# Low parts of routing weights: a GpSimd subtraction or an adding DMA

## The chip, the cores and the metric

The kernel runs on one core of one Trainium2 chip. The metric is the device time of that core in microseconds. Three runs of the kernel before took 2883.79 us in the median (2883.66 to 2886.31).

## The reference

Two blocks follow one another on 512 tokens of width 1024, all in float32. The first holds a layer with a gated convolution and a recurrent mixer, and a layer of sparse attention. The second holds a small mixer, the expert layer to which the change belongs, and a last gate. The expert layer, cut to what matters:

```
q = (xb @ w_q).reshape(T, 8, 2, 128)              # 8 heads, two queries of 128 each
s = jnp.einsum('thpd,hpkd->thpk', q, sub_keys)    # against 2 x 128 keys
sv, si = lax.top_k(s, 16)
cand = sv[:, :, 0, :, None] + sv[:, :, 1, None, :]     # 16 x 16 pairs
cidx = si[:, :, 0, :, None] * 128 + si[:, :, 1, None, :]
top_s, pos = lax.top_k(cand, 16)
eidx = jnp.take_along_axis(cidx, pos, axis=-1)    # 16 of 16384 experts a head
gate = softmax(top_s)
act = gelu(jnp.einsum('thkd,td->thk', expert_u[eidx], xb))
out = jnp.einsum('thk,thkd->td', gate * act, expert_v[eidx])
```

Each token takes 128 experts. An expert is a row of `expert_u`, a row of `expert_v` and a gate.

## The kernel before

**Split products.** TensorE multiplies each float32 matrix as two rounded parts. A weight `w` becomes a high part `wh` (`w` rounded to the matmul's format) and a low part `wl = w - wh`; the activations are split in the same way. `product()` (L214) then issues three matmuls for each k-tile of 128 rows: `wh`·`xh` (L216), `wh`·`xl` (L217) and `wl`·`xh` (L218). `proj()` (L231) runs over the k-tiles of one block of 128 output channels, `KR` of them for each piece of weight that `weight()` (L179) brings.

**Two ways to make the parts.** `weight()` has two branches. In the second one, which the routing stage uses before the change, SP's queue loads the piece as `wraw` (128x256, `KR` = 2, `RB` = 6 buffers; while the experts are routed one more of the name `wrawx` from the pool `wx`), ScalarE copies it to `wh` with rounding (L207), and GpSimd subtracts (L209). The first one is taken where `self.wd` is a pool: SP's queue loads `draw` (128x512, three buffers), ScalarE writes the rounded weight to `dh` (L190) and its negative, rounded too, to `dl` (L191), and a DMA that GpSimd issues (L192) reads the same weight from memory again and adds it to `dl` on arrival. `dh` and `dl` have four buffers each. The convolution stage at the start of the program uses it, with `KR` = 4; behind that stage it is switched off.

**The expert layer.** `peer()` (L1174) treats the first 352 tokens as a dense problem and the last 160 by gathering rows.

- *Routing.* `route()` (L1391) goes over 8 heads. Each has two query projections of 8 k-tiles (`wq2`), scores against the keys, the choice of 16 on VectorE (`tops`), the sums of pairs, and the selection of the indices by comparisons (VectorE L1469, GpSimd L1472, VectorE L1475 and L1476). From the second head on one *early expert* is computed for each projection (`ahead`, `UQ` = 1).
- *Early experts.* 32 of the 128 blocks of `expert_u` (`uT`, 8 k-tiles each) are multiplied before the expert loop: `u_phase` (L1188) runs the projection and a gelu (L1191), the result goes to memory (`ga`, L1200) and is read back later (L1222).
- *Gathered tokens.* `rows()` (L1327) issues an indirect DMA on GpSimd's queue for 128 rows of `expert_u` (`grow`, five buffers, 0.52 MB), VectorE multiplies and sums (L1345). 160 such steps and 160 for `expert_v` (L1361) are spread over the routing stage and the expert loop. `chosen()` (L1309) makes their indices (L1312, L1314).
- *One-hot stage.* The gates become a softmax (L1486 to L1493). Then 44 sets of eight tokens follow: two comparisons on VectorE (`o1` L1511 in float32, `ob` L1514 in bfloat16), the gates laid over one of them by ScalarE (L1519) and GpSimd (L1520), a product on TensorE (L1525), which ScalarE copies to `st` (L1528). SP's queue writes `st` to memory as `gs` (L1529), 11 times 2 MB.
- *Expert loop.* For 128 experts `g4`, four experts' gates, is read back from `gs` on ScalarE's queue (L1219), the gelu is multiplied by it (L1226), split (L241, L242), and multiplied by the block of `expert_v` (`vraw` L1233, `vh` L1236, `vl` on GpSimd L1240 or VectorE L1238), L1256 to L1258. The pool `vp` of this loop lies where the routing stage's pools have been.

**What sets the order.** The program is written in the order of this code, then class `Order` (L1559) reads its dependences, prices each instruction (`cost()`, L1586) and writes an order for every engine's queue by list scheduling; `impose()` (L1859) puts the instructions into it. A DMA of GpSimd is priced there at 1038 ns of GpSimd and by its bytes. The order is made anew for each program, so an edit in one place can move instructions on every engine.

Of the kernel before, what the change touches and what calls it, by code (L numbers as in the profile page):

```python
# [133 lines left out]
class Net:  # L134
# [247 lines left out]
    wi, wxn, wx = -1, 0, None  # L382
# [791 lines left out]
    def peer(self):  # L1174
        nc, tc, I = self.nc, self.tc, self.I
        self.pair.close()
        self.psum2 = None
        with ExitStack() as L:
            self.px = L.enter_context(tc.tile_pool(name="px", bufs=1, space=bass.MemoryType.PSUM))
            hp = L.enter_context(tc.tile_pool(name="hp3", bufs=1))  # L1180
            xh, xl = self.hilo(hp, 8, "x", self.TD)
            dr = L.enter_context(tc.tile_pool(name="pdr", bufs=1, space=bass.MemoryType.DRAM))
            gs = dr.tile([self.TD // 32, 128, 128, 32], F32, name="gs")
            ga = dr.tile([self.NS, 128, self.TD], F32, name="ga")
            self.gather_open(L)
            up = L.enter_context(tc.tile_pool(name="up", bufs=1))

            def u_phase(e, keep):  # L1188
                ps = self.proj(I["uT"][e], xh, xl)
                g = up.tile([128, self.TD], F32, name="ga", bufs=self.GA) if keep else ps  # L1190
                nc.scalar.activation(g, ps, AF.Gelu_apprx_tanh)  # L1191
                return g

            with ExitStack() as RT:
                self.wx, self.wxn = RT.enter_context(tc.tile_pool(name="wx", bufs=1)), self.PX
                early = sorted(range(128), key=lambda e: (e % 4 + 4 * (e // 4 % 2) * (e % 4 == 1), e))[:self.NS]

                def ahead():
                    for i, e in enumerate(early):
                        nc.scalar.dma_start(ga[i], u_phase(e, True))  # L1200
                        self.pull(self.GE)
                        yield
                ahead = ahead()
                self.route(RT, xh, xl, gs, ahead)
                for _ in ahead:
                    pass
                self.wxn = 0
            with ExitStack() as VP:
                vp = VP.enter_context(tc.tile_pool(name="vp", bufs=1))
                g4 = None  # L1210
                GV = self.GV

                def prep(e0):
                    nonlocal g4
                    wh, wl, vh, vl = [], [], [], []
                    for e in range(e0, min(128, e0 + GV)):
                        if e % 4 == 0:
                            g4 = vp.tile([128, self.TD // 32, 4, 32], F32, name="g4", bufs=2)
                            nc.scalar.dma_start(g4, gs[:, :, e:e + 4, :].rearrange("g k e t -> k g e t"))  # L1219
                        if e in early:  # L1220
                            g = up.tile([128, self.TD], F32, name="ga", bufs=self.GA)
                            nc.scalar.dma_start(g, ga[early.index(e)])  # L1222
                        else:
                            g = u_phase(e, False)
                        gv = g.rearrange("p (g t) -> p g t", t=32)
                        nc.vector.tensor_tensor(gv, gv, g4[:, :, e % 4, :], OP.mult)  # L1226
                        h = vp.tile([128, self.TD], F32R, name="wwh", bufs=self.BW)
                        l = vp.tile([128, self.TD], F32R, name="wwl", bufs=self.BW)
                        self.split(h, l, g)
                        wh.append(h)  # L1230
                        wl.append(l)
                        raw = vp.tile([128, 1024], F32, name="vraw", bufs=2)
                        nc.sync.dma_start(raw, I["ev"][e])  # L1233
                        h = vp.tile([128, 1024], F32R, name="vh", bufs=self.BV)
                        l = vp.tile([128, 1024], F32R, name="vl", bufs=self.BV)
                        nc.scalar.activation(h, raw, AF.Copy)  # L1236
                        if e % 8 in self.VD:
                            nc.vector.tensor_tensor(l, raw, h.bitcast(F32), OP.subtract)  # L1238
                        else:
                            nc.gpsimd.tensor_tensor(l, raw, h.bitcast(F32), OP.subtract)  # L1240
                            self.pool = self.last()
                        self.pull(self.GR)
                        vh.append(h)
                        vl.append(l)
                    return wh, wl, vh, vl

                nxt = prep(0)
                for e0 in range(0, 128, GV):
                    wh, wl, vh, vl = nxt
                    if e0 + GV < 128:  # L1250
                        nxt = prep(e0 + GV)
                    for m in range(8):
                        po = self.bank(("xu", "tp", "xu", "nb")[m % 4])[:, 0:self.TD]
                        s = slice(128 * m, 128 * m + 128)
                        for i in range(len(wh)):
                            nc.tensor.matmul(po, vh[i][:, s], wh[i], start=(i == 0), stop=False)  # L1256
                            nc.tensor.matmul(po, vh[i][:, s], wl[i], start=False, stop=False)  # L1257
                            nc.tensor.matmul(po, vl[i][:, s], wh[i], start=False, stop=(i == len(wh) - 1))  # L1258
                        xm = self.x[m][:, 0:self.TD]
                        nc.vector.tensor_tensor(xm, po, xm, OP.add)  # L1260
                self.pull(999)
                self.gather_close()
# [642 lines left out]
```

## Time and profile before

| | before |
|---|---|
| median of 3 runs | 2883.79 us (2883.66 to 2886.31) |
| the profiled execution | 2893.17 us, its span 2891.4 us |
| TensorE matmuls, weight loads | 2621.8 us (91% of the span), 2231.9 us (77%) |
| VectorE | 2247.7 us (78%) |
| ScalarE | 1474.0 us (51%) |
| GpSimd | 1852.7 us (64%) |
| moved by DMA | 552.23 MB, 191 GB/s in the mean |

Shares of busy time are means over the whole span. The expert layer lies between about 1460 and 2750 us. The stretches there have other limits than the mean tells, so the table by stretch in the first group of rows is the first thing to read. PE is TensorE, PEld its weight loads, DVE VectorE, ACT ScalarE, POOL GpSimd, SP SyncE; "ACTq" and "SPq" are the DMA queues of those engines.

### The profile page before, as it was taken

To read this page: it belongs to the slowest core of one execution; us is meant where nothing else is said; L and a number is where in the kernel's file an instruction comes from. 1 tells how busy PE (TensorE), PEld (TensorE's weight loads), DVE (VectorE), ACT (ScalarE), POOL (GpSimd) and SP (SyncE) were. 2 spreads that over 40 slices of the span, in tenths; PEclk is the share of its full clock that TensorE was granted. 3 is DMA by queue.
4 is the path that set the end of the run, shared out by engine and by line. 5 is a ranking of instruction groups with operands and counts; after the bars stand their busy time and mean duration, and the time that the engine had idled before them with its cause. 6 is when DMAs were issued, how large, how long until landed. Compare 5 with 4: busy or idle time off the path is not lost.

```text
span 2891.4 us, 45285 instructions
## 1 busy us (share of the span) xinstructions
PE 2621.8 (91%) x14523; PEld 2231.9 (77%) x14523; DVE 2247.7 (78%) x4338; ACT 1474.0 (51%) x3068; POOL 1852.7 (64%) x1942
## 2 busy tenths in 40 slices
PE   5788998879979999999999988769999999999996
PEld 3656655656757787877878787669999999999995
DVE  6688679896367999973669969978877778788865
ACT  6536546556635538975454347723333444433435
POOL 4535646452245553346657788869988899998963
PEclk9759888888989999999999999979999999999988
DMA  8635444445694231123334366699999999999971
GB/s 264 161 66 118 98 95 107 93 99 126 145 289 143 76 96 44 46 93 105 96 102 148 101 201 245 254 316 337 321 329 314 300 340 339 334 345 320 325 245 64
DMA packets 353440, 552.23 MB, mean 191 GB/s; under 512 B 60081, under 2 KB 239153, under 8 KB 351538
## 3 DMA queue, kind: packets, MB, share of 16 engines
q1 hardware_dynamic: 224690, 295.22, 32.1%
q0 software_dynamic: 64800, 201.88, 23.5%
q10 hardware_dynamic: 63712, 52.24, 5.7%
q8 instruction: 114, 1.87, 0.3%
q14 instruction: 124, 1.02, 0.1%
HBM read 507.76 MB, written 41.42 MB: 190 GB/s over the span
## 4 chain that ended last, share of the span: by engine, by line
PE 31%; DVE 11%; issue 4%; POOL 4%; DMA 2%; ACT 1%; DVEq 0%; POOLq 0%; ACTq 0%; SPq 0%
PE mm L216 5%; PE mm L218 5%; PE mm L217 5%; PE xu L1258 2%; PE xu L1256 2%; PE xu L1257 2%; PE tp L1256 1%; PE tp L1258 1%; POOL wl L209 1%; PE tp L1257 1%; PE nb L1258 1%; PE nb L1256 1%; POOL grow L1330 1%; PE nb L1257 1%; DVE o L1511 1%
## 5 line engine op out<-in xcount | busy, mean ns | idle before, releaser
L209 POOL TENSOR_TENSOR wl<-wraw,wh 128x256 fp32r<-128x256 f32 x937 | 776.7, 846 | 349.3 <-ACT wh L207 290.4
L207 ACT ACTIVATE wh<-wraw 128x256 fp32r<-128x256 f32 x937 | 367.5, 413 | 466.2 <-PE mm L217 235.1
L216 PE MATMUL mm<-xh,wh 128*128 128x352 f32 (+1 forms) x1464 | 512.1, 350 | 11.2 <-DVE wwl L242 3.5
L218 PE MATMUL mm<-xh,wl 128*128 128x352 f32 (+1 forms) x1464 | 506.1, 349 | 6.7 <-POOL wl L209 6.7
L217 PE MATMUL mm<-xl,wh 128*128 128x352 f32 (+1 forms) x1464 | 507.9, 348 | 2.7 <-DVE xl L287 1.8
L216 PEld LDWEIGHTS mm<-xh,wh 128*128 128x128 f32 x1464 | 278.7, 190 | 33.8 <-DVE gate L1544 4.3
L218 PEld LDWEIGHTS mm<-xh,wl 128*128 128x128 f32 x1464 | 277.4, 190 | 26.5 <-POOL wl L209 8.6
L217 PEld LDWEIGHTS mm<-xl,wh 128*128 128x128 f32 x1464 | 278.5, 190 | 24.2 <-DVE xl L287 3.8
L1240 POOL TENSOR_TENSOR vl<-vraw,vh 128x1024 fp32r<-128x1024 f32 x96 | 231.2, 2416 | 6.0 <-ACT vh L1236 4.4
L192 POOL DMA_DIRECT2D dl<-in_wev x114 | 102.4, 917 | 201.7 <-ACT dl L191 180.5
L1345 DVE SCALAR_TENSOR_TENSOR gscr<-grow,wide 128x1024 bf16<-128x1024 f32 x160 | 194.1, 1213 | 38.3 <-DMA grow<-in_ue,gidx 34.8
L216 PE MATMUL mm<-xh,dh 128*128 128x512 f32 x456 | 205.5, 453 | 14.9 <-ACT xh L355 9.6
L1361 DVE SCALAR_TENSOR_TENSOR wide<-grow,gdot,wide 128x1024 f32<-128x1024 f32 x158 | 202.3, 1280 | 12.3 <-DMA grow<-in_ev,gidx 11.2
L217 PE MATMUL mm<-xl,dh 128*128 128x512 f32 x456 | 202.7, 446 | 9.2 <-DVE xl L356 9.2
L218 PE MATMUL mm<-xh,dl 128*128 128x512 f32 x456 | 202.0, 446 | 9.1 <-DMA dl<-in_wev 9.1
L1330 POOL DMA_INDIRECT grow<-in_ue,gidx x160 | 161.1, 1007 | 64.7 <-DVE gscr L1345 31.1
L1256 PE MATMUL xu<-wwh,vh 128*128 128x352 f32 x512 | 167.4, 328 | 32.2 <-ACT wwh L241 28.0
L1330 POOL DMA_INDIRECT grow<-in_ev,gidx x160 | 157.4, 984 | 36.1 <-issue 23.5
L1258 PE MATMUL xu<-wwh,vl 128*128 128x352 f32 x512 | 167.4, 328 | 9.7 <-POOL vl L1240 7.7
L1191 ACT ACTIVATE mm<-mm 128x352 f32<-128x352 f32 x96 | 43.0, 448 | 253.0 <-PE mm L218 211.4
L1257 PE MATMUL xu<-wwl,vh 128*128 128x352 f32 x512 | 167.2, 327 | 0.4 <-DVE wwl L242 0.4
L780 DVE SCALAR_TENSOR_TENSOR x<-u,vec,x 128x512 f32<-128x512 f32 x152 | 165.6, 1089 | 2.4
(575 smaller groups left out, 6961.2 us busy)
## 6 DMA issues: line engine op xcount, KB each, us to landing
vraw<-in_ev SPq DMA_DIRECT2D x128, 512.0 KB
wraw<-in_uT SPq DMA_DIRECT2D x494, 128.0 KB
draw<-in_wev SPq DMA_DIRECT2D x114, 256.0 KB
dl<-in_wev POOLq DMA_DIRECT2D x114, 256.0 KB
gs<-st SPq DMA_DIRECT2D x11, 2048.0 KB
g<-gs ACTq DMA_DIRECT2D x32, 704.0 KB
wraw<-in_wod SPq DMA_DIRECT2D x156, 128.0 KB
adaw<-in_adaT SPq DMA_DIRECT2D x32, 512.0 KB
```

What stands on the lines that cost most here:

```text
L207: nc.scalar.activation(wh, raw[:, s], AF.Copy)
L209: nc.gpsimd.tensor_tensor(wl, raw[:, s], wh.bitcast(F32), OP.subtract)
L216: nc.tensor.matmul(ps, wh, xh, start=start, stop=False)
L217: nc.tensor.matmul(ps, wh, xl, start=False, stop=False)
L218: nc.tensor.matmul(ps, wl, xh, start=False, stop=stop)
L1240: nc.gpsimd.tensor_tensor(l, raw, h.bitcast(F32), OP.subtract)
L1256: nc.tensor.matmul(po, vh[i][:, s], wh[i], start=(i == 0), stop=False)
L1257: nc.tensor.matmul(po, vh[i][:, s], wl[i], start=False, stop=False)
L1258: nc.tensor.matmul(po, vl[i][:, s], wh[i], start=False, stop=(i == len(wh) - 1))
L1330: self.nc.gpsimd.indirect_dma_start(out=t, out_offset=None, in_=src, in_offset=bass.IndirectOffsetOnAxis(ap=self.gidx[i][:, k:k + 1], axis=0))
L1345: nc.vector.scalar_tensor_tensor(scr, u, 1.0, x, op0=OP.mult, op1=OP.mult, accum_out=self.gdot[i][:, k:k + 1])
L1361: nc.vector.scalar_tensor_tensor(acc, r, w, acc, op0=OP.mult, op1=OP.add)
```

## The change

For the routing stage the change takes the first branch of `weight()` in place of the second: the pool `wr` holds `draw`, `dh` and `dl`, and `KR` is 4. Behind the early experts it is switched off again. The extra buffer `wrawx` goes.

```diff
             with ExitStack() as RT:
-                self.wx, self.wxn = RT.enter_context(tc.tile_pool(name="wx", bufs=1)), self.PX
+                self.wd, self.KR = RT.enter_context(tc.tile_pool(name="wr", bufs=1)), 4
                 early = sorted(range(128), key=lambda e: (e % 4 + 4 * (e // 4 % 2) * (e % 4 == 1), e))[:self.NS]
...
                 for _ in ahead:
                     pass
-                self.wxn = 0
+                self.wd, self.KR = None, 2
```

The query weights and the early experts' weights are 16 and 32 blocks of 8 k-tiles. Before, that is 192 pieces of 128x256, each with a load, a copy on ScalarE and a subtraction on GpSimd. Now it is 96 pieces of 128x512, each with a load, two copies on ScalarE and a second, adding DMA on GpSimd's queue.

`Order` writes another order for all engines. Three places of it follow. In a row stand the line, the operation, what it writes and reads, the size, and how many follow one another.

On VectorE, from the last selection (L1476) to the first one-hot comparison (L1511), with L1345 a gathered row's product, before:

```order
L1312 SCALAR_TENSOR_TENSOR gsrc<-sel 128x16 x6
L1345 SCALAR_TENSOR_TENSOR gscr,gdot_14764<-grow,wide 128x1024 x3
L1486 COPY top<-sel 128x32
L1496 CAST keys<-iota 128x512
L1487 TENSOR_TENSOR sel<-sel,top 128x512
L1491 TENSOR_REDUCE sm<-sel 128x32
L1345 SCALAR_TENSOR_TENSOR gscr,gdot_14764<-grow,wide 128x1024
L1492 RECIPROCAL sm<-sm 128x32
L1345 SCALAR_TENSOR_TENSOR gscr,gdot_14764<-grow,wide 128x1024
L1493 TENSOR_TENSOR sel<-sel,sm 128x512
L1345 SCALAR_TENSOR_TENSOR gscr,gdot_14764<-grow,wide 128x1024
L1511 TENSOR_TENSOR o_17562<-iota,kt 128x1024
```

and now:

```order
L1476 TENSOR_REDUCE sel<-eq 128x4x16 x2
L1345 SCALAR_TENSOR_TENSOR gscr,gdot_14764<-grow,wide 128x1024
L1486 COPY top<-sel 128x32
L1496 CAST keys<-iota 128x512
L1487 TENSOR_TENSOR sel<-sel,top 128x512
L1314 COPY gidx_14766<-gsrc 128x16
L1312 SCALAR_TENSOR_TENSOR gsrc<-sel 128x16 x3
L1314 COPY gidx_14766<-gsrc 128x16 x2
...
L1493 TENSOR_TENSOR sel<-sel,sm 128x512
L1345 SCALAR_TENSOR_TENSOR gscr,gdot_14764<-grow,wide 128x1024
L1371 COPY gate_17246<-sel 128x128
L1511 TENSOR_TENSOR o_17262<-iota,kt 128x1024
```

Between the last selection and the first one-hot comparison there are two gather products now, and eight before; ahead of the last selection six now, and three before. The early experts' matmuls between the last scores and the first one-hot product are 166 now, and 379 before.

On GpSimd, behind the last one-hot operation (L1520), where L1330 issues a gather, before:

```order
L1520 TENSOR_TENSOR o_18548<-ob,kt 128x512
L1330 DMA grow<-in_ue,gidx_14766 128x1024 x3
L209 TENSOR_TENSOR wl<-wraw,wh 128x256 x2
L1330 DMA grow<-in_ue,gidx_14766 128x1024 x9
L1240 TENSOR_TENSOR vl<-vraw,vh 128x1024
```

and now:

```order
L1520 TENSOR_TENSOR o_18248<-ob,kt 128x512
L192 DMA dl<-in_uT 128x512
L1330 DMA grow<-in_ue,gidx_14766 128x1024 x3
L192 DMA dl<-in_uT 128x512
L1330 DMA grow<-in_ue,gidx_14766 128x1024
L192 DMA dl<-in_uT 128x512
...
L192 DMA dl<-in_uT 128x512
L1330 DMA grow<-in_ue,gidx_14766 128x1024
L192 DMA dl<-in_uT 128x512
L1330 DMA grow<-in_ue,gidx_14766 128x1024 x2
L209 TENSOR_TENSOR wl<-wraw,wh 128x256
```

Of the 96 adding DMAs 69 stand ahead of the last selection's product on GpSimd (L1472), 18 in the one-hot stage and 9 here, with 16 gathers between and behind them.

On ScalarE, at the first load of g (L1219), before:

```order
L1528 ACTIVATE st<-xu 128x128x4
L207 ACTIVATE wh<-wraw 128x256 x2
L1191 ACTIVATE mm<-mm 128x352
L1219 DMA g_19656<-gs 128x11x128
L1219 DMA g_19886<-gs 128x11x128
```

and now:

```order
L190 ACTIVATE dh<-draw 128x512
L1191 ACTIVATE ga<-mm 128x352
L191 ACTIVATE dl<-draw 128x512
L1200 DMA ga<-ga 128x352
L1191 ACTIVATE ga<-mm 128x352
L1200 DMA ga<-ga 128x352
L207 ACTIVATE wh<-wraw 128x256 x4
L1191 ACTIVATE mm<-mm 128x352
L1219 DMA g_19176<-gs 128x11x128
```

The load of g stands behind the early experts' last gelus now. Between the last one-hot product and the loop's first product (L1256) TensorE has 144 matmuls now, and 12 before; ahead of the loop's first product the k-tiles of expert weights are 272 in both.

## Rows read from the trace of the kernel before

**Rows 1.** Stretch, us; busy PE, PEld, DVE, ACT, POOL (count); clock, DMA share, GB/s.

```profile
1494.00:1689.00 195.00, 181.39 (x970) 160.45 (x970) 192.06 (x950) 79.25 (x196) 142.41 (x173) 0.98 0.40 122
1689.00:1731.00 42.00, 37.71 (x221) 36.73 (x220) 16.74 (x41) 20.98 (x52) 32.18 (x43) 0.96 0.73 228
1731.00:1874.00 143.00, 115.78 (x854) 106.85 (x853) 136.71 (x118) 112.71 (x302) 124.22 (x88) 0.98 0.66 246
1874.00:1903.00 29.00, 1.31 (x8) 1.02 (x7) 14.48 (x25) 4.28 (x9) 14.47 (x14) 0.56 1.03 379
1903.00:2750.00 847.00, 827.99 (x5040) 821.55 (x5040) 684.82 (x984) 331.25 (x700) 754.24 (x709) 0.99 0.95 325
```

**Rows 2.** Groups: subtractions from 1460 to 1700 us; adding DMA issues, whole span.

```profile
L209 POOL TENSOR_TENSOR wl<-wraw,wh 128x256 fp32r<-128x256 f32 x146 | 112.0, 788 | 31.1 <-ACT wh L207 25.2 <-PE mm L218 3.7 <-PE mm L217 2.1
...
L192 POOL DMA_DIRECT2D dl<-in_wev x114 | 102.4, 917 | 201.7 <-ACT dl L191 180.5
```

**Rows 3.** VectorE in order of time, 1676 to 1800 us: start, duration, [idle before].

```profile
1687.13 0.57 DVE L1476 TENSOR_REDUCE sel<-eq 128x64 f32<-128x256 bf16 x1
...
1694.39 0.59 DVE L1312 SCALAR_TENSOR_TENSOR gsrc<-sel 128x16 int32<-128x16 f32 x6
...
1699.87 1.22 DVE L1345 SCALAR_TENSOR_TENSOR gscr<-grow,wide 128x1024 bf16<-128x1024 f32 x1 [4.88 <-DMA grow<-in_ue,gidx]
1701.02 0.08 DVE L1345 DVE_READ_ACCUMULATOR gscr<-grow,wide 128x1 f32 x1
...
1710.22 1.22 DVE L1345 SCALAR_TENSOR_TENSOR gscr<-grow,wide 128x1024 bf16<-128x1024 f32 x1 [9.12 <-DMA grow<-in_ue,gidx]
...
1720.22 0.19 DVE L1486 COPY top<-sel 128x32 f32<-128x32 f32 x1 [1.68 <-ACT wh L207]
```

**Rows 4.** GpSimd in order of time, 1676 to 1735 us: two gathers issued.

```profile
1694.34 0.98 POOL L1330 DMA_INDIRECT grow<-in_ue,gidx  x1
...
1703.14 0.96 POOL L1330 DMA_INDIRECT grow<-in_ue,gidx  x1
```

**Rows 5.** The one-hot comparison: shortest/median/longest ns; groups from 1731 to 1874 us.

```profile
L1511 DVE TENSOR_TENSOR o<-iota,kt x44: 1210/1214/4164, 1730.7 to 1869.1; 128x1024 f32<-128x1024 f32 x44
...
L1511 DVE TENSOR_TENSOR o<-iota,kt 128x1024 f32<-128x1024 f32 x44 | 66.5, 1514 | 1.6 <-PE xu L1525 1.6
...
L209 POOL TENSOR_TENSOR wl<-wraw,wh 128x256 fp32r<-128x256 f32 x25 | 31.2, 1259 | 1.2 <-ACT wh L207 1.1
```

**Rows 6.** All engines in order of time, 1866 to 1930 us.

```profile
1872.30 0.97 POOL L1330 DMA_INDIRECT grow<-in_ue,gidx  x1 [0.51 <-DVE gscr L1345]
...
1883.36 6.39 ACTq L1219 DMA_DIRECT2D g<-gs  x2
1884.05 1.22 DVE L1345 SCALAR_TENSOR_TENSOR gscr<-grow,wide 128x1024 bf16<-128x1024 f32 x1 [5.70 <-DMA grow<-in_ue,gidx]
...
1901.15 0.53 DVE L1226 TENSOR_TENSOR mm<-mm,g 128x352 f32<-128x352 f32 x1 [4.54 <-DMA g<-gs]
...
1902.69 0.66 PE L1256 MATMUL xu<-wwh,vh 128*128 128x352 f32 x1 [27.69 <-ACT wwh L241]
```

**Rows 7.** DMA queues, 200 to 700 us: packets, MB, share; then the issues.

```profile
q0 software_dynamic: 10825, 19.72, 25.0%
q1 hardware_dynamic: 36462, 31.47, 23.6%
...
dl<-in_wev POOLq DMA_DIRECT2D x76, 256.0 KB
```

**Rows 8.** DMA queue of GpSimd, 1874 to 1903 us.

```profile
q0 software_dynamic: 1718, 6.28, 57.7%
```

**Rows 9.** TensorE in order of time, 1690 to 1880 us: first and last of 14.

```profile
1724.71 0.33 PE L216 MATMUL mm<-xh,wh 128*128 128x352 f32 x1
...
1726.84 0.32 PE L217 MATMUL mm<-xl,wh 128*128 128x352 f32 x1
```

**Rows 10.** Waits of TensorE, 1903 to 2800 us: sum, count, longest, us.

```profile
PE xu L1258 <- POOL vl L1240: 7.7, 6, 3.6
```

## The prediction

> **What bounds the kernel now.** I read the table by stages first, then the groups of the routing stage, the order of time on VectorE and GpSimd around the end of routing, the wait before the expert loop, and the DMA queues. In the table [rows 1] the reader is to see five stretches with different limits. While the eight heads are routed (1494 to 1689 us) VectorE is busy 192.1 of 195 us. From 1689 to 1731 no compute engine but TensorE is full. In the one-hot stage (1731 to 1874) VectorE has 136.7 of 143 us. From 1874 to 1903 TensorE stands still and the DMA engines are at 1.03. In the expert loop TensorE has 828 of 847 us, with DMA at 0.95. TensorE's matmuls up to the loop's first product are the same in number in both programs (272 k-tiles of expert weights ahead of it), and behind it TensorE is full. So what the change is worth is the shift of that first product, 1902.69 us in this run [rows 6], and what the loop then adds.
>
> **The change part by part.**
>
> *GpSimd's subtractions.* 192 subtractions leave, 112.0 us of them (146) between 1460 and 1700 us alone; 96 issues of 917 ns, 88 us, come instead [rows 2]. GpSimd limits neither the routed heads nor the expert loop by itself, so this pays only where somebody waits for it.
>
> *From the last selection to the first one-hot comparison, 1687.7 to 1730.7 us, 43.0 us* [rows 3, 5]. VectorE stands 4.88 and 9.12 us for gathered rows, and from 1695.0 to 1720.2 us it does three gather products and nothing else. GpSimd issues those gathers at 1694.34 and 1703.14, among its subtractions [rows 4]. In the new order six gather products stand ahead of the last selection in place of three, and two behind it in place of eight. Of the 43.0 us the 25.2 us of the three products leave, and three more products of 1.30 us (1.22 us and 0.08 for the sum); three products and one that stays in that place cost 3.9 + 1.3 us ahead. That is -25.2 - 3.9 + 5.2, rounded with a little less waiting for the rest: -26 us. Bounds: -5, if the transposes behind 157 early matmuls come late (their 13 blocks of 512 columns have to land first), and -31, if nothing waits.
>
> *The routed heads.* 69 of the 96 adding transfers lie ahead of the last selection. In the convolution stage 76 of them took 25.0% of 16 engines in 500 us, 1.64 us each, and plain loads 3.75 us per MB [rows 7]. 65 of them, less four at the mixer's end, are 107 us in a stretch of 195 us whose DMA share is 0.40: it goes to 0.95. TensorE has some slack against VectorE there. I take +5 us for weights that come late, between 0 and +14.
>
> *The one-hot stage.* It stays VectorE's: 44 pairs of comparisons. The f32 comparison takes 1214 ns in the median, 1514 ns in the mean [rows 5], 13 us over 44 of them; in the stage GpSimd does 25 subtractions of 1259 ns beside its own products. The slow cases also come beside those products, which stay, so I take -4 us, between 0 and -13. The Trainium skill (SBUF — State Buffer, "Who interferes with whom") says that a VectorE instruction with two SBUF inputs contends with a GpSimd instruction that reads SBUF, and not with one that only writes it; by that an issue of a transfer leaves VectorE alone, the whole 13 us could come, and the sum would be -2 us. The trace agrees as far as that issues do not grow (917 ns in the mean), and cannot show the rest. DMA there has room: 0.66, with 18 adding transfers of 1.64 us about 0.85.
>
> So the last one-hot product would come 25 us earlier (-26 + 5 - 4).
>
> *The wait before the expert loop, 28.7 us now (from the end of the one-hot stage at 1874.0 to 1902.69).* After the last one-hot product a block of gs is written and read back as g; the load of g is issued at 1883.36 us and used at 1901.15 us, 17.8 us later, with DMA full [rows 6]. The new order puts much more here. GpSimd has 9 adding transfers and 16 gathers in turn, then the subtractions of the next experts; VectorE has 24 gather products ahead of the first use of g in place of 12; ScalarE issues the load of g behind the early experts' last products; TensorE has 144 matmuls in place of 12. In DMA time: 9 x 1.64 = 14.8 us; 8 blocks of raw weights, 0.98 us each, 7.9 us; 6 more loads of 128 KB, 2.9 us; 12 more gathers, 1.39 us each (57.7% of 29 us for 12.0 gathers of 0.52 MB [rows 8]), 16.7 us; two vraw loads less, -3.9 us. That is +38 us of full DMA time on a stretch that is already full. A gather issued at 1872.30 is used at 1884.05, after a stand of 5.70 us [rows 6], so the queue is what they wait for. The lower bound is TensorE's own work, 144 x 0.164 us (14 matmuls, 13 steps in 2.13 us [rows 9]) = 23.6 us, and then a load of g of 17.8 us: 41.4 us, +13. The upper is +38 and a late load of g, +45. The stretch is the one that the trace shows full, so I stay near the sum: +34 us. The Trainium skill (DMA: Bandwidth & Descriptors, "Anatomy of one DMA — SWDGE (gpsimd) path") fits a transfer of GpSimd's queue as 2.0 us and its bytes over 436 GB/s; by that an adding transfer of 256 KB moves its data in 0.60 us, by estimate, in place of 1.64 us, the wait would be some 9 us shorter and the sum -2 us. The rows of the convolution stage decide here: 1.64 us.
>
> *The expert loop.* 11 gathers more are done when it starts. TensorE waits in it 7.7 us for GpSimd's vl [rows 10]; I take -2 us, between 0 and -8.
>
> **Sum:** -26 + 5 - 4 + 34 - 2 = +7 us. The profiled execution took 2893.17 us (span 2891.4 us and 1.8 us around it) and would take 2900; it is 9.4 us above the median of the runs, 2883.79 us. I forecast 2891 us, 0.24% above. What a measurement of this kernel can tell from no change is about 0.2%, 5.8 us.
>
> **The rivals.**
>
> *The wait stays short (faster).* The load of g is the mechanism. If the early weights land ahead of the last one-hot product, the wait is the 41.4 us of the lower bound, +13, and the sum is -26 + 5 - 4 + 13 - 2 = -14 us; with no delay in the routed heads -19. The time is 2870 us (2860 to 2880). The point from which it decides: the wait ends less than 50 us after the last one-hot product. For it: the loads of raw weights can run ahead by three blocks, and the one-hot stage has DMA time free. Against it: GpSimd's queue is in order, and its last adding transfer stands behind 14 gathers that wait for buffers.
>
> *DMA binds from the heads on (slower by more).* The share of 0.95 in the routed heads makes weights late by 9 us more, the first one-hot comparison comes only some 12 us earlier, and the wait is 70 us. -26 + 14 - 0 + 41 - 2 = +27 us, 2911 us (2900 to 2930). For it: the price of 1.64 us, 1.7 times the 0.98 us of a plain load of the same size; against it: VectorE's backlog in the heads, which hides late weights.
>
> *The gain and the loss even out.* The same terms with a wait of 55 us give -1 us. It is the lower part of the forecast's own range, 2881 to 2900 us.
>
> **How the numbers follow.** The forecast has 0.45, the short wait 0.28, the DMA-bound case 0.27. The forecast's own range lies 0.25 within 0.2% and 0.20 above; of the short wait 0.27 is faster and 0.01 within; the DMA-bound case is slower. So faster 0.27, within 0.2% 0.26, slower 0.47. The range leaves out about a tenth on each side: 2866 to 2912 us.
>
> **What would show it.** Right: the first one-hot comparison some 15 to 30 us earlier against the last selection, with no stand of VectorE for gathers there; the one-hot stage at 135 to 145 us; TensorE at work, in pieces, in a wait of 55 to 70 us between the last one-hot product and the loop's first; the load of g issued more than 30 us after that product. Wrong: adding transfers well under 1.64 us, a load of g that is issued at once, or a first one-hot comparison that comes no earlier; and an expert loop that is shorter or longer by more than 8 us, of which nothing above speaks.

## The result, and the profile after

The changed kernel takes 2908.72 us in the median of 11 runs, the kernel before 2886.31 us in as many: a ratio of 1.0068 (95% interval 1.0048 to 1.0088). That is 19.6 us slower by the ratio; the medians lie 22.4 us apart. The profiled execution took 2908.72 us, 15.6 us more than the one of before, which stood 6.9 us above its median: the stages below add up to the 15.6 us. The sign is the one that was forecast and the time lies in the range; the size is nearly three times the 7 us of the sum. The stages tell why.

| stage (from, to) | before, us | after, us | change | forecast |
|---|---|---|---|---|
| routed heads (first product with the keys, last selection) | 189.5 | 190.4 | +0.9 | +5 |
| last selection, first one-hot comparison | 43.0 | 10.9 | -32.1 | -26 |
| one-hot stage (first comparison, last product) | 142.4 | 139.5 | -2.9 | -4 |
| wait (last one-hot product, first product of the expert loop) | 29.6 | 53.8 | +24.2 | +34 |
| expert loop (first product, last) | 904.1 | 934.4 | **+30.3** | **-2** |
| behind the loop | 84.5 | 80.8 | -3.7 | 0 |

The loop's first product comes at 1891.72 us, 11.0 us earlier than before [rows 6], and not later, as the forecast had it. All of the loss lies in the loop, between its first and its last product.

The table by stretch of the changed kernel (columns: stretch, its length, busy time of PE, PEld, DVE, ACT, POOL with the count of instructions, clock, DMA share, GB/s):

```profile
1494.00:1687.50 193.50, 179.22 (x961) 155.07 (x960) 184.98 (x961) 102.09 (x198) 100.34 (x107) 1.00 0.93 216
1687.50:1698.40 10.90, 7.05 (x41) 5.93 (x39) 6.22 (x25) 7.64 (x12) 8.22 (x9) 1.00 1.03 279
1698.40:1838.00 139.60, 123.26 (x904) 116.33 (x904) 133.04 (x129) 120.37 (x310) 107.76 (x79) 0.96 0.88 294
1838.00:1891.70 53.70, 29.55 (x144) 26.70 (x142) 23.97 (x40) 13.40 (x29) 29.73 (x33) 0.79 1.06 359
1891.70:2826.10 934.40, 890.70 (x5347) 879.23 (x5348) 744.65 (x1020) 352.61 (x735) 782.85 (x743) 0.98 0.90 307
```

The same view of the kernel before, cut to its loop:

```profile
1902.70:2806.80 904.10, 882.25 (x5347) 873.33 (x5348) 726.86 (x1041) 348.44 (x734) 799.26 (x751) 0.99 0.94 321
```

In the heads the DMA share goes from 0.40 [rows 1] to 0.93, as forecast, and the stage keeps its length. In the loop TensorE has the same 5347 matmuls, but stands 934.4 - 890.7 = 43.7 us in place of 904.1 - 882.25 = 21.9 us, and its busy time is 8.4 us longer, at a granted clock of 0.98 in the mean in place of 0.99. The DMA engines are not busier there: their share falls from 0.94 to 0.90.

VectorE in order of time between the last selection and the first comparison of the changed kernel (start, duration, idle time before):

```profile
1686.36 1.17 DVE L1476 TENSOR_REDUCE sel<-eq 128x64 f32<-128x256 bf16 x2
1687.44 1.21 DVE L1345 SCALAR_TENSOR_TENSOR gscr<-grow,wide 128x1024 bf16<-128x1024 f32 x1
...
1691.82 0.69 DVE L1493 TENSOR_TENSOR sel<-sel,sm 128x512 f32<-128x512 f32 x1
1697.13 1.22 DVE L1345 SCALAR_TENSOR_TENSOR gscr<-grow,wide 128x1024 bf16<-128x1024 f32 x1 [4.62 <-DMA grow<-in_ue,gidx]
...
1698.42 1.22 DVE L1511 TENSOR_TENSOR o<-iota,kt 128x1024 f32<-128x1024 f32 x1
```

Two gather products stand here and one of them is waited for, 4.62 us; before there were eight [rows 3].

What TensorE waits for in the loop (sum, count, longest, in us), after:

```profile
PE xu L1256 <- DVE x L1260: 24.6, 14, 6.0
PE xu L1256 <- ACT wwh L241: 9.6, 1, 9.6
PE xu L1258 <- POOL vl L1240: 5.2, 6, 1.4
PE xu L1258 <- DVE vl L1238: 5.2, 2, 2.6
```

The same view of the kernel before, for the first of these:

```profile
PE xu L1256 <- DVE x L1260: 3.4, 2, 3.0
```

(The 9.6 us for `wwh` stand ahead of the loop's first product and belong to the wait.) The additions of L1260 empty TensorE's banks, and the wait for them grows by 21.2 us, about as much as TensorE's whole standing does (21.8 us). They may be late because VectorE is held by other work that stands ahead of them in its queue; gamult_pool below tests that. The groups of VectorE in the loop, after (busy us, mean ns, idle time before and what ended it):

```profile
L1238 DVE TENSOR_TENSOR vl<-vraw,vh 128x1024 fp32r<-128x1024 f32 x32 | 81.6, 2551 | 6.6 <-ACT vh L1236 4.1 <-issue 2.3
L1226 DVE TENSOR_TENSOR ga<-ga,g 128x352 f32<-128x352 f32 x31 | 56.0, 1808 | 33.6 <-DMA g<-gs 33.2 <-DMA wraw<-in_uT 0.5
L1226 DVE TENSOR_TENSOR mm<-mm,g 128x352 f32<-128x352 f32 x94 | 49.6, 528 | 60.4 <-ACT mm L1191 59.7
```

and before:

```profile
L1238 DVE TENSOR_TENSOR vl<-vraw,vh 128x1024 fp32r<-128x1024 f32 x31 | 59.4, 1918 | 11.9 <-ACT vh L1236 7.4 <-issue 4.0 <-POOL vl L1240 0.5
L1226 DVE TENSOR_TENSOR ga<-ga,g 128x352 f32<-128x352 f32 x31 | 37.4, 1207 | 12.9 <-issue 7.8 <-DMA g<-gs 5.1
```

The multiplication by g has one size in both of its rows. With the gelu in PSUM (`mm`) it takes 528 ns; for the early experts, with both inputs in SBUF (`ga`), 1808 ns in the mean, 1207 before. Taken at 0.52 us each, 31 of them hold VectorE 40 us too long after, 21 us before; the stand ahead of them grows by 20.7 us, that for g alone by 28.1 us; and the subtractions L1238 take 633 ns more each, some 20 us over 32. (A few instructions are missing from the traces: 31 stand for 32.) One place of the loop shows beside what they are stretched:

```profile
2385.51 0.52 DVE L1260 TENSOR_TENSOR x<-nb,x 128x352 f32<-128x352 f32 x1
2385.94 8.59 DVE L1226 TENSOR_TENSOR ga<-ga,g 128x352 f32<-128x352 f32 x1
2394.45 0.52 DVE L1226 TENSOR_TENSOR mm<-mm,g 128x352 f32<-128x352 f32 x1
```

GpSimd in the same microseconds:

```profile
2385.01 0.94 POOL L1330 DMA_INDIRECT grow<-in_ev,gidx  x1 [1.33 <-DMA wraw<-in_uT]
2385.95 4.75 POOL L1240 TENSOR_TENSOR vl<-vraw,vh 128x1024 fp32r<-128x1024 f32 x2
2390.65 3.49 POOL L209 TENSOR_TENSOR wl<-wraw,wh 128x256 fp32r<-128x256 f32 x5
```

Seven subtractions stand back to back on GpSimd from 2385.95 to 2394.14 us, and an instruction of VectorE of half a microsecond lasts from 2385.94 to 2394.53. This is the longest case. Elsewhere VectorE gets in while the run goes on, as here behind two subtractions:

```profile
2296.12 4.69 DVE L1226 TENSOR_TENSOR ga<-ga,g 128x352 f32<-128x352 f32 x1
2295.59 4.75 POOL L1240 TENSOR_TENSOR vl<-vraw,vh 128x1024 fp32r<-128x1024 f32 x2
2300.31 3.17 POOL L209 TENSOR_TENSOR wl<-wraw,wh 128x256 fp32r<-128x256 f32 x4
```

Of the 31 multiplications of this kind in the trace of the loop 19 took more than 0.7 us. Eight of them ended 0.4 us behind the last subtraction of a run, 11 ended 0.4 to 0.5 us behind a subtraction after which the run went on. So the theory to test: **the order that the planner wrote for the loop is worse** (A), because VectorE meets such instructions where GpSimd runs without a gap and where g has not landed. The rival: **the adding transfers leave the loop in a worse state**, whatever its order (B).

### The profile page after: what moved, and what is told of

Its sections match the earlier page's. It is cut to its first block, busy times and chain, and to the rows that moved or that the text cites. A ratio compares the mean times of both kernels' runs of the same rounds, so it can differ in the third digit from the quotient of the medians.

```text
span 2907.0 us, 44899 instructions
## 1 busy us (share of the span) xinstructions
PE 2624.6 (90%) x14523; PEld 2228.5 (77%) x14523; DVE 2257.6 (78%) x4338; ACT 1507.7 (52%) x3068; POOL 1771.8 (61%) x1846
## 5 line engine op out<-in xcount | busy, mean ns | idle before, releaser
L209 POOL TENSOR_TENSOR wl<-wraw,wh 128x256 fp32r<-128x256 f32 x772 | 637.2, 843 | 342.8 <-ACT wh L207 272.5
L216 PE MATMUL mm<-xh,wh 128*128 128x352 f32 (+1 forms) x1208 | 426.7, 354 | 10.7 <-DVE wwl L242 4.1
L218 PE MATMUL mm<-xh,wl 128*128 128x352 f32 (+1 forms) x1208 | 424.4, 352 | 2.1 <-POOL wl L209 2.1
L217 PE MATMUL mm<-xl,wh 128*128 128x352 f32 (+1 forms) x1208 | 423.2, 351 | 1.8 <-DVE xl L287 1.7
L218 PE MATMUL mm<-xh,dl 128*128 128x512 f32 (+1 forms) x712 | 290.1, 410 | 28.9 <-DMA dl<-in_uT 21.9
L216 PE MATMUL mm<-xh,dh 128*128 128x512 f32 (+1 forms) x712 | 291.7, 411 | 19.8 <-ACT xh L355 10.2
L217 PE MATMUL mm<-xl,dh 128*128 128x512 f32 (+1 forms) x712 | 288.7, 407 | 9.0 <-DVE xl L356 9.0
L1345 DVE SCALAR_TENSOR_TENSOR gscr<-grow,wide 128x1024 bf16<-128x1024 f32 x160 | 194.2, 1214 | 37.3 <-DMA grow<-in_ue,gidx 35.2
L190 ACT ACTIVATE dh<-draw 128x512 fp32r<-128x512 f32 x226 | 141.0, 626 | 145.0 <-PE mm L217 125.1
L1330 POOL DMA_INDIRECT grow<-in_ue,gidx x160 | 163.0, 1019 | 70.2 <-DVE gscr L1345 42.0
L1256 PE MATMUL xu<-wwh,vh 128*128 128x352 f32 x512 | 170.8, 334 | 34.2 <-DVE x L1260 24.6
L218 PEld LDWEIGHTS mm<-xh,dl 128*128 128x128 f32 x712 | 146.8, 206 | 60.4 <-DMA dl<-in_uT 28.0
L1330 POOL DMA_INDIRECT grow<-in_ev,gidx x160 | 153.1, 957 | 62.5 <-DVE wide L1361 21.2
L216 PEld LDWEIGHTS mm<-xh,dh 128*128 128x128 f32 x712 | 146.0, 205 | 46.7 <-ACT xh L355 13.7
```

What stands on the lines that cost most here:

```text
L190: nc.scalar.activation(wh, raw, AF.Copy)
L209: nc.gpsimd.tensor_tensor(wl, raw[:, s], wh.bitcast(F32), OP.subtract)
L216: nc.tensor.matmul(ps, wh, xh, start=start, stop=False)
L217: nc.tensor.matmul(ps, wh, xl, start=False, stop=False)
L218: nc.tensor.matmul(ps, wl, xh, start=False, stop=stop)
L1330: self.nc.gpsimd.indirect_dma_start(out=t, out_offset=None, in_=src, in_offset=bass.IndirectOffsetOnAxis(ap=self.gidx[i][:, k:k + 1], axis=0))
```

## The experiments

Stages of all runs, from one profiled execution each, and the ratio of the timed runs to the kernel before (an execution can stand up to 16 us from the median of its kernel, so the last column decides on totals):

| kernel | heads | to first one-hot | one-hot | wait | loop | ratio (95%) |
|---|---|---|---|---|---|---|
| before | 189.5 | 43.0 | 142.4 | 29.6 | 904.1 | 1 |
| the changed kernel | 190.4 | 10.9 | 139.5 | 53.8 | 934.4 | 1.0068 (1.0048 to 1.0088) |
| add_oldloop | 191.9 | 12.0 | 139.5 | 53.3 | 917.6 | 0.9988 (0.9969 to 1.0007) |
| sub_newloop | 190.0 | 42.3 | 142.1 | 30.3 | 957.2 | 1.0130 (1.0104 to 1.0155) |
| add_query | 198.7 | 11.7 | 144.7 | 41.8 | 905.2 | 1.0008 (0.9986 to 1.0030) |
| add_early | 193.1 | 12.9 | 138.2 | 54.1 | 895.5 | 0.9949 (0.9931 to 0.9967) |
| gamult_pool | 189.5 | 11.7 | 140.2 | 56.3 | 914.4 | 1.0046 (1.0019 to 1.0073) |
| vl_act | 190.1 | 11.5 | 138.1 | 53.6 | 899.4 | 0.9914 (0.9887 to 0.9941) |
| dl_plain | 182.6 | 6.4 | 139.1 | 52.4 | 931.7 | 1.0009 (0.9987 to 1.0031) |
| sub_512 | 201.9 | 12.6 | 144.7 | 46.0 | 910.3 | 1.0035 (1.0015 to 1.0054) |
| before_p100 | 191.3 | 11.9 | 140.6 | 55.3 | 903.0 | 1.0038 (1.0020 to 1.0056) |
| after_p100 | 190.8 | 15.8 | 141.8 | 57.3 | 906.9 | 1.0061 (1.0036 to 1.0085) |
| before_p200 | 187.2 | 41.4 | 141.8 | 35.1 | 905.6 | 1.0090 (1.0057 to 1.0123) |
| after_p200 | 199.8 | 12.8 | 136.5 | 58.6 | 915.3 | 1.0067 (1.0042 to 1.0091) |

**The two orders crossed: add_oldloop and sub_newloop.** Behind the loop's first product both programs consist of the same instructions. So each program can be given the other's order from there on. Both programs are planned, their instructions are matched in the order of the code (the routing stage's weight pieces, which differ, are all done by then), and the queue is cut at the first product:

```diff
+def join(a, oa, ob, m):
+    loop = next(k for k, n in enumerate(oa) if a.c[n][0] == "PE" and any(a.tag.get(t, ("", ""))[1] == "vh" for t in a.ins[n]))
+    place = {n: k for k, n in enumerate(ob)}
+    want = oa[:loop] + sorted(oa[loop:], key=lambda n: place[m[n]])
...
-    nc = build(A, Order(build(A)).best()[1])
+    nc = build(A, plan(A))
```

> The changed kernel with its own order up to the expert loop's first product, and from there on the order of the kernel before. Theory A (the new order of the loop costs the time: VectorE meets the multiplication by g too early and stands there, and the sums that free TensorE's banks wait behind it): the loop, from its first to its last product, goes from 933 us back to 895 to 908 us, and since the first product comes about 11 us earlier than before, the ratio to before is 0.990 to 0.999. Theory B (the routing stage leaves the loop in a worse state, transfers still under way, so the loop is long in any order): the loop stays at 925 us or more and the ratio at 1.004 to 1.010.

> The kernel before, with subtractions and its own order up to the expert loop's first product, and from there on the order of the changed kernel; no adding transfer is in the routing stage. Theory A (order of the loop): the loop takes 925 to 940 us in place of 901, the ratio to before is 1.008 to 1.015. Theory B (state that the routing leaves): the loop stays within 8 us of 901 and the ratio is 0.997 to 1.004.

The changed kernel in the old loop order has a ratio of 0.9988, which takes back all of the loss: 1.0068 - 0.9988 is 0.8%, 23 us. The loop is 917.6 us, 10 us more than A gave, in an execution that stood 9.5 us above its median. The kernel before in the new loop order has 1.0130, with no adding transfer anywhere in its routing stage, and 957.2 us in the loop, longer even than A's 925 to 940, in an execution that stood 15.7 us above its median. What TensorE and VectorE show of the crossed kernels goes with the order and not with the routing stage. add_oldloop:

```profile
PE xu L1259 <- DVE x L1263: 9.0, 4, 2.7
L1241 DVE TENSOR_TENSOR vl<-vraw,vh 128x1024 fp32r<-128x1024 f32 x32 | 56.1, 1754 | 15.6 <-DMA wraw<-in_uT 7.5 <-issue 4.4 <-ACT vh L1239 1.9
L1229 DVE TENSOR_TENSOR ga<-ga,g 128x352 f32<-128x352 f32 x32 | 37.1, 1159 | 16.6 <-DMA g<-gs 16.2 <-issue 0.4
```

sub_newloop:

```profile
PE xu L1259 <- DVE x L1263: 31.1, 11, 6.3
L1241 DVE TENSOR_TENSOR vl<-vraw,vh 128x1024 fp32r<-128x1024 f32 x31 | 76.4, 2466 | 7.4 <-ACT vh L1239 4.6 <-issue 2.7
L1229 DVE TENSOR_TENSOR ga<-ga,g 128x352 f32<-128x352 f32 x31 | 55.7, 1798 | 41.8 <-DMA g<-gs 33.5 <-DMA vraw<-in_ev 8.3
```

9.0 us against 31.1 us of TensorE's waiting for the additions, 1159 ns against 1798 ns for the multiplications, and 16.2 against 33.5 us of standing for g. That the loop's order makes the loss is shown, and B has fallen; by what in the order is the next question. (Lines are three higher in these kernels.) The four kernels also price the routing stage of the change by itself: with the old order of the loop it is worth 0.9988, not clear of nothing, and with the new one 1.0068 / 1.0130 = 0.994. Apart from the loop's order the change costs nothing that these runs can tell.

**What in the order holds VectorE: gamult_pool and vl_act.** Both keep the changed kernel's order instruction for instruction and alter one operation of the loop.

```diff
# gamult_pool
-                        nc.vector.tensor_tensor(gv, gv, g4[:, :, e % 4, :], OP.mult)
+                        (nc.gpsimd if e in early else nc.vector).tensor_tensor(gv, gv, g4[:, :, e % 4, :], OP.mult)
# vl_act
-                            nc.gpsimd.tensor_tensor(l, raw, h.bitcast(F32), OP.subtract)
+                            nc.scalar.activation(l, raw, AF.Copy)
```

> The changed kernel in its own order, instruction for instruction, with one edit: the 32 multiplications by g that read two tiles of SBUF (the early experts', re-read from memory) are done by GpSimd in place of VectorE. Theory A1 (those multiplications hold VectorE: it stands 33.6 us ahead of them and their own time is stretched by 40.4 us over 32, while GpSimd runs subtractions back to back, and the sums that free TensorE's banks queue behind): VectorE's part of that goes, the loop falls from 934 us to 900 to 918 us, ratio to before 0.992 to 1.002. Theory A2 (the order loses its time elsewhere, and these multiplications stand in slack): the loop stays at 925 us or more, ratio 1.004 to 1.012, more if GpSimd's wait for g delays its subtractions.

> The changed kernel in its own order, with one edit: the 96 low parts vl of the loop that GpSimd subtracts (2.41 us each) are written by a ScalarE copy; the subtraction is left out, 96 of the 128 blocks of expert_v get a wrong low part. If GpSimd's long runs stretch VectorE's two-SBUF operations, the 32 multiplications' stretch falls from 40.4 us to under 12 us, the 32 subtractions of VectorE (2.55 us in the mean) fall to about 1.3 us, and the loop falls to 890 to 915 us although ScalarE has 102 us more to do: ratio 0.988 to 1.000. If the long times are waits for the loads of g, the stretch stays above 30 us and the loop within 8 us of 934 us.

gamult_pool gave the loop of A1, 914.4 us, but not its ratio: 1.0046, only 0.2% better than the changed kernel, and the two intervals overlap. The profiled execution stood 6.9 us below its kernel's median, so the loop looks shorter there than it mostly is. TensorE's wait for the additions goes from 24.6 to 1.8 us, so these multiplications, with the stand for g ahead of them, are what made the additions late; a part of the gain came back as another wait, that for GpSimd's vl, 16.9 us in place of 5.2:

```profile
PE xu L1256 <- DVE x L1260: 1.8, 2, 1.5
PE xu L1258 <- POOL vl L1240: 16.9, 14, 3.2
```

GpSimd takes 948 ns for a multiplication that VectorE does in 0.52 us when it is let alone, 30 us over the 32 (the line's instructions: shortest, median, longest, ns):

```profile
L1226 POOL TENSOR_TENSOR ga<-ga,g x32: 926/948/1006, 1893.9 to 2752.9; 128x352 f32<-128x352 f32 x32
```

vl_act takes the 96 long subtractions from GpSimd. Its groups on VectorE, behind TensorE's wait for the additions (three lines lower in its kernel):

```profile
PE xu L1259 <- DVE x L1263: 15.5, 5, 7.3
L1238 DVE TENSOR_TENSOR vl<-vraw,vh 128x1024 fp32r<-128x1024 f32 x32 | 40.8, 1274 | 9.7 <-ACT vh L1236 9.5
L1226 DVE TENSOR_TENSOR ga<-ga,g 128x352 f32<-128x352 f32 x31 | 18.9, 611 | 51.1 <-DMA g<-gs 51.1
```

The same multiplications take 611 ns in place of 1808, the subtractions 1274 in place of 2551, and the ratio is 0.9914, 1.5% below the changed kernel's, though ScalarE has 89 us more to do. So the long times came with GpSimd's subtractions and were not waits for loads. The stand for g does not go, it grows from 33.2 to 51.1 us, and TensorE still waits 15.5 us for additions in place of 24.6. So the stretch alone does not explain that wait; what the stand for g costs by itself no run here prices. Nor do these runs say how much of the difference between the two orders is this stretch: the order of before has 21 us of it too, vl_act was made of the changed kernel alone, and it takes 230 us of subtractions from GpSimd, which may help in other ways.

**The price of adding: dl_plain.** The same order again, and a plain write in place of the adding one.

```diff
-            nc.gpsimd.dma_start(wl, src, accum_op=OP.add)
+            nc.gpsimd.dma_start(wl, src.bitcast(F32R))
```

> The changed kernel in its own order, with one edit: in the routing stage the second DMA of a weight writes it to dl without adding, so the low parts of the query and early experts' weights are wrong (the weight itself in their place). It prices the adding. If the adding makes a transfer cost 1.64 us of full DMA time and a plain one about 1 us, the share of GpSimd's queue in the routed heads falls from 58% to about 40%, the wait before the loop of 53.8 us falls by 4 to 8 us, ratio to before 1.003 to 1.006. If the adding costs nothing against a plain load, both stay, ratio 1.005 to 1.009.

1.0009, 0.6% or 17 us below the changed kernel: more than was expected, and in another place. The wait before the loop falls by 1.4 us only, the heads by 7.8 and the way to the first one-hot by 4.5. (The changed kernel, add_oldloop, gamult_pool and vl_act have the same work in the same order up to the loop; between them the wait differs by 3.0 us, the heads by 2.4 and the way to the first one-hot by 1.1.) In the heads TensorE waits 13.8 us for low parts in the changed kernel (first two rows) and 6.0 in dl_plain (last two, five lines lower in its kernel):

```profile
PE mm L218 <- DMA dl<-in_uT: 7.6, 11, 1.6
PE mm L218 <- DMA dl<-in_wq: 6.2, 7, 1.4
PE mm L223 <- DMA dl<-in_wq: 4.3, 4, 2.0
PE mm L223 <- DMA dl<-in_uT: 1.7, 3, 1.2
```

So the adding has a price of its own, of about the size of that of the loop's order; other parts of the change give it back, since apart from the loop's order the crossed kernels show no loss. GpSimd's DMA queue between 1494 and 1687 us (share of 16 engines; then issues) in the changed kernel:

```profile
q0 software_dynamic: 10401, 20.78, 58.2%
...
dl<-in_uT POOLq DMA_DIRECT2D x39, 256.0 KB, 6.5
dl<-in_wq POOLq DMA_DIRECT2D x28, 256.0 KB, 5.4
grow<-in_ue,gidx POOLq DMA_INDIRECT x7, 8.1
```

and in dl_plain:

```profile
q0 software_dynamic: 11396, 23.61, 40.8%
...
dl<-in_uT POOLq DMA_DIRECT2D x43, 256.0 KB, 4.7
dl<-in_wq POOLq DMA_DIRECT2D x27, 256.0 KB, 3.8
grow<-in_ue,gidx POOLq DMA_INDIRECT x13, 6.4
```

These shares are 112.3 and 78.7 us of the 193. Less 1.39 us for each gather [rows 8], a price from another stretch, 67 adding transfers take 112.3 - 9.7 us, 1.53 us each, and 70 plain ones 78.7 - 18.1 us, 0.87 us each: estimates both.

**Parts of the change: add_query, add_early, sub_512.** The adding DMA for the query weights alone, for the early experts alone, and the larger pieces with GpSimd's subtraction. Each is planned anew.

```diff
# add_query, in route(); self.wr is the pool "wr" of the change
+                    self.wd, self.KR = self.wr, 4
                     ps = self.proj(I["wq2"][2 * h + z], gh, gl)
+                    self.wd, self.KR = None, 2
# add_early, in ahead()
+                        self.wd, self.KR = wr, 4
                         nc.scalar.dma_start(ga[i], u_phase(e, True))
+                        self.wd, self.KR = None, 2
# sub_512, in weight(), on top of the change, in the routing stage
-            nc.scalar.activation(wl, raw, AF.Copy, scale=-1.0)
-            nc.gpsimd.dma_start(wl, src, accum_op=OP.add)
+            nc.gpsimd.tensor_tensor(wl, raw, wh.bitcast(F32), OP.subtract)
+            self.pool = self.last()
```

> Adding transfers for the query weights alone (32 of the 96), subtraction for the early experts; the order is made anew. If each adding transfer costs (1.64 us of full DMA time where DMA is full), few of them fall there: ratio 0.996 to 1.001, the wait before the loop within 5 us of the 29.6 us of before. If a new order of the loop decides, the ratio follows the length of the loop, 901 us in before and 933 us in the changed kernel, whichever it is here.

> Adding transfers for the early experts' weights alone (64 of the 96), subtraction for the query weights; the order is made anew. If the transfers cost, the wait before the loop is 45 to 60 us as in the changed kernel and the ratio 1.002 to 1.009. If a new order of the loop decides, the ratio follows the length of the loop between 901 and 933 us, and a wait of 45 us or more with a loop near 901 us gives 0.994 to 1.000.

> Pieces of 128x512 in the routing stage as in the changed kernel, but with GpSimd's subtraction in place of the adding DMA; the order is made anew. If the shorter way from the last selection to the first one-hot (43.0 us before, 10.9 us in the changed kernel) comes from the DMA that takes GpSimd's work over, it is back at 30 us or more here. If it comes from the larger pieces or the new order, it is under 20 us. The time follows the length of the loop that the new order gives: 0.990 to 1.010.

add_early, with 64 of the 96 adding transfers, is the fastest whole kernel: 0.9949, below both, although its wait is 54.1 us as in the changed kernel. Its loop is 895.5 us. add_query has a loop of 905.2 us and 1.0008. In these two the ratio goes with the loop and the start of it, not with the number of transfers. How much of add_early's gain is its own and how much a lucky order stays open: only one order of it was run. sub_512 has no adding transfer and yet comes from the last selection to the first comparison in 12.6 us, so that way can be short without the DMA; its heads are 11.5 us longer than the changed kernel's.

**Other orders of the same two kernels.** The planner keeps the best of four weights with three rounds each, by its own prices. Two of the orders that it throws away:

```diff
-    nc = build(A, Order(build(A)).best()[1])
+    nc = build(A, Order(build(A)).best(alphas=(100,))[1])
# and, as the p200 kernels
+    nc = build(A, Order(build(A)).best(alphas=(200,), rounds=1)[1])
```

> The kernel before, with another of the orders that its own planner writes (weight 100 alone in place of the best of four). Theory A (the order of the loop makes the difference, and which order comes out is chance): the loop lies anywhere from 890 to 940 us and the ratio to before between 0.990 to 1.015, following the loop and the wait ahead of it. Theory B (the adding transfers themselves make the changed kernel slower): another order alone moves the kernel by less than 0.3%.

> The changed kernel with the planner's order at weight 100 alone. Theory A: the first product of the loop comes 5 to 15 us earlier than in the kernel before in its own order, the loop again lies anywhere from 890 to 940 us, and the pair with the kernel before at weight 100 does not have to stand as the first pair does (1.0068). Theory B: 1.004 to 1.010 of the kernel before at the same weight.

> The kernel before, with the planner's order at weight 200 after one round backwards. Theory A: the loop from 890 to 940 us, the ratio to before 0.990 to 1.015. Theory B: within 0.3% of before.

> The changed kernel with the planner's order at weight 200 after one round backwards. Theory A: loop from 890 to 940 us, and over the three pairs the sign of the difference to the kernel before is not the same. Theory B: 1.004 to 1.010 of the kernel before at the same weight.

With not a line of its computation changed, the kernel before is 0.4% and 0.9% slower, the second clear of the 0.3% that B allows. Pair by pair the change gives 1.0068, then 1.0061 / 1.0038 = 1.0023, then 1.0067 / 1.0090 = 0.9977: the mean is 0.2%, and the spread between orders is as large as the effect that was measured. That the sign differs, as A has it, is not shown: from the runs of the second and the third pair the 95% intervals are about 0.2% and 0.4% on either side, so neither is clear of no difference. B's 1.004 to 1.010 lies above both. Where the p100 orders lose is not the loop, though: its lengths are 903.0 and 906.9 us, and the first product with the keys comes at 1518.7 and 1517.4 us in place of 1498.2 and 1497.2, so 20 us are gone ahead of the routing stage. Nor is it the loop in before_p200, 905.6 us: its first product comes 7.6 us later and the part behind the loop is 7.3 us longer than in the kernel before. So which order comes out makes a difference, but A's account of it, that the ratio follows the loop and the wait, does not hold in these runs. And before_p100, with 256-wide pieces and GpSimd's subtractions, has 11.9 us from the last selection to the first comparison and a wait of 55.3 us, the very shape that the prediction put down to the change:

```profile
1709.40 0.60 DVE L1476 TENSOR_REDUCE sel<-eq 128x64 f32<-128x256 bf16 x1
...
1718.12 1.21 DVE L1345 SCALAR_TENSOR_TENSOR gscr<-grow,wide 128x1024 bf16<-128x1024 f32 x1
...
1721.93 1.23 DVE L1511 TENSOR_TENSOR o<-iota,kt 128x1024 f32<-128x1024 f32 x1
```

## Why the prediction was right, and where it was wrong

- **The sign and the range** held: 2883.79 x 1.0068 is 2903 us, between 2866 and 2912. The reason that was given for the sign did not, and the sign was luck: the wait was to cost more than the earlier one-hot stage brings; it cost less, TensorE reached the loop 11.0 us earlier, and with the loop's old order (add_oldloop) nothing of the loss is left.
- **The step that failed: the expert loop.** The term was -2 us, between 0 and -8, because the loop has the same matmuls and 11 gathers fewer. It was +30.3 us. Only the waits of before for vl were priced [rows 10], as if the loop kept its order. The planner wrote the loop anew as well, and that order cost 23 us by add_oldloop. TensorE's longer wait in it was for additions behind VectorE's two-SBUF multiplications, as gamult_pool shows; how much of the 23 us these make stays open. The text had named a loop longer by 8 us as what would make it wrong, without a mechanism for it.
- **The last selection to the first one-hot**: -32.1 us, forecast -26, 1 us beyond its bounds of -5 to -31. What was read from the order, two gather products in place of eight, was right; the sign that VectorE would stand for none of them was not, it stood 4.62 us for one. But the short way belongs to the order: sub_512 and before_p100 have it with subtractions.
- **The routed heads**: +0.9 us, forecast +5 between 0 and +14. The DMA share of 0.93 was forecast as 0.95. dl_plain shows that the late weights do cost there, 7.8 us; the heads of dl_plain are 6.9 us shorter than those of before, so something else in the stage, not found here, gives about as much back.
- **The price of an adding transfer**: 1.64 us was taken from the convolution stage, 1.53 us are worked out in the heads, 0.1 us less.
- **The one-hot stage**: -2.9 us for -4, for the wrong reason. The comparison did not get faster by losing GpSimd's 25 subtractions beside it, 1562 ns in the mean in place of 1514 [rows 5]:

```profile
L1511 DVE TENSOR_TENSOR o<-iota,kt 128x1024 f32<-128x1024 f32 x44 | 68.5, 1562 | 3.6 <-PE xu L1525 3.6
```

- **The wait**: +24.2 us for +34, between +13 and +45. TensorE's 144 matmuls are there, and so is the full DMA (1.06); the matmuls took 29.6 us where the lower bound had 23.6, at a granted clock of 0.79 in the stretch. The load of g is issued 39.1 us after the last one-hot product's end at 1837.9, as forecast (more than 30), but TensorE's first product comes 14.7 us behind it, sooner than the 19.3 us of before [rows 6]; the sum had added all transfers of the stretch up as if g had to wait for each of them. dl_plain moved the wait by 1.4 us only, so the adding was not what made it long.

```profile
1877.03 0.40 ACTq L1219 DMA_DIRECT2D g<-gs  x1
...
1891.72 0.66 PE L1256 MATMUL xu<-wwh,vh 128*128 128x352 f32 x1 [9.57 <-ACT wwh L241]
```

- **The rivals**: the short wait (under 50 us) did not come, 53.8 us; the DMA-bound case came nearer to the size, 27 us, by a mechanism that did not come: the heads were 0.9 us longer and not 14, and the wait was not 70 us. The wait is that of the third rival, 55 us, in which gain and loss even out; without the loop's new order the result would have been close to that.

## What to carry to other kernels

Where a planner writes the order, an edit in one stage is an edit of every stage behind it: compare the new order there as well, and separate the two effects by giving one program the other's order from a point at which both have done the same work. An effect under 1% is to be measured over several orders of both kernels before it is put down to the edit. An instruction of VectorE that reads two tiles of SBUF is to be priced by what GpSimd does beside it: here 0.5 us in a gap or with one input in PSUM, and up to 8.6 us beside a run of subtractions.

## What the runs showed of the hardware

- A multiplication of VectorE of 0.52 us took 8.59 us beside a run of seven subtractions on GpSimd, to within 0.4 us of the run's end, so it can sit through six boundaries between gapless GpSimd instructions. It does not always: 11 of the 19 stretched multiplications of that loop got in at a boundary inside a run, 0.4 to 0.5 us behind it, and the subtraction that followed then took about 1.1 us in place of 0.7. What decides at which boundary is open. With the 96 long subtractions gone from GpSimd the mean fell from 1808 to 611 ns. The Trainium skill (SBUF — State Buffer, "Who interferes with whom") says that a VectorE instruction with two SBUF inputs contends with a GpSimd instruction that reads SBUF; the trace agrees, and the same instruction with one input in PSUM stays at 527 to 530 ns in all of these runs.
- An adding DMA of 256 KB took 1.53 us of the 16 engines in the mean, a plain one 0.87 us, both worked out from the queue's share in the heads, and the whole kernel took 0.6% more with 96 of the first in place of 96 of the second.
